# Element-wise steps between GpSimd and VectorE, and the listed order at a layer's end, in a two-layer decoder trunk

## The chip, the core and the metric

One core of one Trainium2 chip runs the whole kernel as one program. The metric is the device time of an execution in microseconds (us). Engines are named as the profile names them: PE is TensorE's matrix multiply, PEld its weight load, DVE VectorE, ACT ScalarE, POOL GpSimd, and SP the engine that issues most of the DMAs.

## What is computed

512 tokens of width 1024 go through two layers. The first mixes tokens by pooling over windows, the second by stick-breaking attention with 16 heads. After each mixer stands a squared-ReLU MLP of width 4096, and every mixer and MLP stands between two RMSNorms. Cut to what matters here:

```python
def rms_norm(x, g):
    return x * lax.rsqrt(jnp.mean(x * x, axis=-1, keepdims=True) + EPS) * g

def sq_relu_mlp(h, w_up, w_down):
    u = jnp.matmul(h, w_up)
    return jnp.matmul(jnp.square(jax.nn.relu(u)), w_down)

for layer in range(2):
    h = rms_norm(x, mix_pre_g[layer])
    m = pool_mixer(h, ...) if layer == 0 else attention(h, k, v) @ w_o
    x = x + rms_norm(m, mix_post_g[layer])
    h = rms_norm(x, mlp_pre_g[layer])
    x = x + rms_norm(sq_relu_mlp(h, w_up[layer], w_down[layer]), mlp_post_g[layer])
    if layer == 0: k, v = split(rms_norm(x, kv_norm_g) @ w_kv)
```

## The kernel before

All products are float32 in three passes: each operand is split into a rounded part (`hi`, a cast on ACT) and the rest (`lo`, a subtraction on DVE), and PE adds hi·hi, hi·lo and lo·hi. So behind nearly every product stand one ACT cast and one DVE subtraction (`split`, line 266, `weight`, line 156).

**The MLP** (`mlp`, from line 575). 32 blocks of 128 hidden channels are made by up products (lines 678 to 680, 24 matmuls a block), squared-ReLU by ACT (lines 596 and 597). 28 of the blocks are taken in five groups of 2, 3, 3, 3 and 3 pairs. Class `Seven` multiplies a group's 2x2 blocks with 7 products in place of 8. Its left operands are blocks `r` and sums of them: four sums per group, made in `left` by GpSimd (line 519). Its right operands are weight halves `w1` and `w2` (the latter in the tile `xn3`) and four combinations `e` and `w12` of them, made in `right` by DVE (line 538). Each product is 18 matmuls for a group of three (line 564), and two additions on DVE take it out of PSUM (line 573). The second half of a group's weights goes into the one tile `xn3` by a DMA of 1.5 MB that waits for the last split of the group before. The last four blocks are multiplied in `contract` (lines 286 to 288, DVE line 426). There each token tile `t` also gets its norm: squares on ACT (line 269), the product with the norm's gain (line 312; of the first 512 columns by GpSimd, of the others by DVE), the sum (line 275) and its power -0.5 on GpSimd (line 282), and the addition to `x` (line 324).

During the first layer's MLP the attention's weights are scaled, split and stored again (`split_apart`, DVE line 216).

**The order.** Where nothing else is said, a scheduler places the instructions of each engine by its own timeline when the program is built; each engine then runs its own queue in that fixed order. Two regions are written by hand for all engines: the pooling (`MIX_ORDER`) and the stretch from the last pair of heads to the second layer's MLP (`END_ORDER`). In `END_ORDER` each word is one step of one engine. `O`, `E`, `F`, `G` are parts of the output projection on PE, with `ov` and `ev` taking them out on DVE (line 1089). `s`, `g`, `V`, `a` are squares (ACT), product with the gain (DVE), factor (DVE line 275, then GpSimd) and addition (DVE) of the first norm; `S`, `W`, `n` the same for the second (`n` is DVE line 363). `t`, `h`, `l` are the transposes (PE), and the split of their result (ACT, DVE line 388). `i`, `k` are the split of an up-weight block 0 to 3 (ACT, DVE line 1139), and `u` is the first half of that block's up product, over token tiles 0 and 1. Digits are the tile and the column half. `ATT_ORDER` lists the attention's steps before: `V` values (24 matmuls a token tile), `P` a pair's queries and keys, `T` transposes, `E1` the hand-written end.

Instructions that the scheduler still owns can be placed between those of a hand-written region: the second layer's first split of `w1` was placed there (line 266).

Of the kernel before, what the change touches and what calls it, by code (L numbers as in the profile page):

```python
# [13 lines left out]
ALU = mybir.AluOpType  # L14
# [18 lines left out]
TS = [slice(t * P, (t + 1) * P) for t in range(T)]  # L33
NS = [slice(0, 512), slice(512, 1024)]
# [24 lines left out]
ATT_ORDER = [  # L59
    (w[0], int(w[1]), [int(c) for c in w[2:]])  # L60
    for w in """V001 K0 V02 P0 V03 S0 P1 T0 V101 S1 A0 P2 T1 V123 A1 S2 P3 T2 O00123 A2 S3 P4 V201 T3 A3
    S4 P5 T4 V223 S5 A4 P6 V301 T5 S6 A5 V323 P7 T6 E1""".split()
]


# [5 lines left out]

END_ORDER = [
    (w if w.startswith("d7") else w.rstrip("0123456789"), [int(c) for c in w if c.isdigit() and not w.startswith("d7")])
    for w in """D6 R0 R1 z01 z00 z02 x00 z11 x02 z12 x01 z10 x12 A60 sc0 x10 y10 A61 y00 oc60 y01 E01 y02 od60 oc61
    mu0 y12 E00 x11 y11 sc1 T01 T02 T00 ah01 O00 ah02 d7h ah00 O01 al01 al00 O10 mu1 O11 ov01 al02 od61
    T12 A70 ah12 ov00 hh6 al12 T11 hl6 T10 ah11 ov11 F00 d7l ah10 al11 O20 oc70 al10 od70 A71 ov20 ov10
    O21 oc71 od71 O30 ov21 hh7 hl7 O31 ov30 G00 ov31 i1 F01 ev00 i0 G01 k1 E11 s00 ev01 R3 F11 g00 s01
    G11 k0 E10 V0 g01 F10 a01 R2 G10 ev11 S01 E20 ev10 s11 a00 s10 F20 g11 G20 S00 V1 g10 E21 ev20 a11
    s20 E31 W0 a10 S11 E30 n01 S10 n00 F30 W1 g20 t01 n11 t00 h01 G30 n10 h00 F31 l01 t10 ev30 G31 h10
    l00 F21 s30 ev31 G21 l10 s31 t11 ev21 h11 g30 s21 l11 i2 V2 u0 V3 g31 i3 a20 a31 S20 a30 S31 u1 g21  # L80
    S30 a21 W3 S21 k2 n31 u2 W2 n30 n21 n20 t30 k3 t21 h30 t20 h21 t31 l30 u3 h20 l21 h31 l20 l31""".split()
]


# [6 lines left out]
def trunk(ctx, tc, x, consts, grow, pw, wup, wdn, wq, wk, wv, wo, out):  # L91
    nc = tc.nc
# [11 lines left out]
    def name(s):  # L104
        uid[0] += 1
        return f"{s}{uid[0]}"

    def ps():
        return psum.tile([P, 512], F32, tag="ps", name=name("ps"))


    xt = [keep.tile([P, D], F32, tag=f"x{t}", name=f"x{t}") for t in range(T)]
# [26 lines left out]
    behind, latest = {}, {}  # L139
# [29 lines left out]
    gate, queue, made, ahead, dn_pool, att_pool = [False], [], {}, 4, [None], [None]  # L169
# [72 lines left out]
    for l in range(2):  # L242
        if l == 1:
            n = len(queue)
# [40 lines left out]
    def mm3(dst, ah, al, bh, bl, start, stop):  # L285
        nc.tensor.matmul(dst, ah, bh, start=start, stop=False)  # L286
        nc.tensor.matmul(dst, ah, bl, start=False, stop=False)  # L287
        nc.tensor.matmul(dst, al, bh, start=False, stop=stop)  # L288
# [9 lines left out]
    class Update:  # L298
# [8 lines left out]
        def squares_of(self, n, y):  # L307
            square_sum(y, self.xn[:, self.cuts[n]], self.st, (0, 1, 4)[n])

        def product(self, n, y, on):  # L310
            cut = self.cuts[n]
            on.tensor_tensor(out=self.scaled[:, cut], in0=y, in1=self.gpost[:, cut], op=ALU.mult)

        def square(self, n, y, on):

            self.squares_of(n, y)
            self.product(n, y, on)

        def first_rstd(self):
            self.r = rstd(self.st, 0, self.eps, third=len(self.cuts) > 2)  # L320
# [11 lines left out]
        def add(self):  # L332
            self.first_rstd()
            for n, cut in enumerate(self.cuts):
                self.add_part(n)
                if self.final:
                    nc.sync.dma_start(out[TS[self.t], cut], xt[self.t][:, cut])
                else:
                    self.squares_of_x(n)

# [62 lines left out]
    def contract(lhs, w, y, first, update=None, tiles=range(T), soon=False):  # L403


        last = len(lhs) - 1
        ups = {}
        for t in tiles:
            up = ups[t] = update(t, y[t]) if update is not None else None
            cuts = up.cuts if up is not None else NS  # L410
            pds = [ps()[:, : cut.stop - cut.start] for cut in cuts]

            def product(n, cs):
                for c in cs:
                    (lh, ll), (wh, wl) = lhs[c], w[c]
                    mm3(
                        pds[n], lh[:, TS[t]], ll[:, TS[t]], wh[:, cuts[n]], wl[:, cuts[n]],
                        c == 0, c == last,
                    )

            def evacuate(n):
                part = y[t][:, cuts[n]]
                if first:
                    nc.scalar.copy(part, pds[n])
                else:
                    nc.vector.tensor_tensor(out=part, in0=pds[n], in1=part, op=ALU.add)
                if up is not None:
                    up.square(n, part, nc.vector if n else nc.gpsimd)

            normed = up is not None and not up.final  # L430
            if t == 0:
                product(0, range(last))
                product(1, range(last))
                product(0, [last])
            else:
                product(0, range(last + 1))
            if normed and t == T - 1 and not soon:
                ups[0].transpose()
            evacuate(0)
            if normed and t > 0:  # L440
                ups[t - 1].rstd()
                ups[t - 1].norm()
            if t == 0:
                product(1, [last])
            elif normed and t == T - 1:
                product(1, [0])
                ups[1].transpose()
                product(1, range(1, last + 1))
            else:
                product(1, range(last + 1))  # L450
                if normed and soon and t == 2:
                    ups[0].transpose()
            evacuate(1)
            for n in range(2, len(cuts)):
                product(n, range(last + 1))
                evacuate(n)
            if up is None:
                fill()
            else:
                up.add()  # L460
                if normed and t == T - 2:
                    behind.update(latest)
        if normed:
            ups[T - 1].rstd()
            ups[T - 1].norm()
            for t in (T - 2, T - 1):
                pending[t] = ups[t]
# [4 lines left out]
    class Seven:  # L472
# [38 lines left out]
        def left(self, i):  # L511

            n, key = self.n, self.PRODUCTS[i][1]
            lo, hi = slice(0, S // 2), slice(S // 2, S)
            r11, r21, r12, r22 = (self.r[:, k, :n, h] for k in range(2) for h in (lo, hi))
            if i == 0:
                self.s1 = self.mp.tile([P, MOST, S // 2], F32, tag="s1", name=name("s1"))
            s1 = self.s1[:, :n]
            sub = lambda out, x, y, op=ALU.subtract: nc.gpsimd.tensor_tensor(out=out, in0=x, in1=y, op=op)  # L519
            if key == "s3":  # L520
                sub(s1, r21, r22, ALU.add)
                sub(r21, r11, r21)
                sub(r11, s1, r11)
            elif key == "r22":
                sub(r11, r12, r11)
            src = {"r11": r11, "s3": r21, "s2": r11, "r22": r22, "s1": s1, "r12": r12, "s4": r11}[key]
            a = self.mp.tile([P, 2, MOST, S // 2], F32R, tag="a", bufs=2, name=name("a"))
            split(src, a[:, 0, :n], a[:, 1, :n])
            return a
# [45 lines left out]
    def mlp(l, mp, update):  # L575

        gate[0] = False
        y = y_tiles()
        firsts = [2 * sum(GROUPS[:g]) for g in range(len(GROUPS))]
        plain = 2 * sum(GROUPS)  # L580
        groups = [Seven(l, firsts[g], n, mp) for g, n in enumerate(GROUPS)]
# [44 lines left out]
        for j, (pu, w) in enumerate(first):  # L626
            up_block(pu, w, slice(S // 2, S))
            up(j, pu)
        for i in range(2):
            groups[0].make(i)  # L630
        for g, group in enumerate(groups):
            coming = groups[g + 1] if g + 1 < len(groups) else None
            if coming:
# [1 line left out]
            ups = list(range(firsts[g + 1], firsts[g + 1] + 2 * GROUPS[g + 1]) if coming else range(plain, NJ))  # L635
# [6 lines left out]
            for i in range(7):  # L642
# [12 lines left out]
                else:  # L655
# [4 lines left out]
                    elif i == 5:  # L660
                        piece = lambda tag, k, bufs=1: mp.tile([P, k, D], F32R, tag=tag, bufs=bufs, name=name("dn"))
                        w, e, x = piece("w1", 3), piece("e", 1), piece("w", 3, 2)
# [5 lines left out]
        w = [get(("dn", l, j)) for j in range(plain, NJ)]  # L668
# [14 lines left out]
    with tc.tile_pool(name="mix0", bufs=1, reuse_waits="tile") as mp:  # L683
# [29 lines left out]
        left, stats, ups, ys, own = {}, {}, {}, {}, {}  # L713
# [100 lines left out]
        def half_up(j):  # L814
# [4 lines left out]
            "z": busy, "r": scale_row, "e": scale_copy, "w": linear, "q": first_squares, "v": first_norm,  # L819
            "b": band, "p": pooled, "c": copied, "f": reached, "m": mixed,  # L820
            "s": lambda t, h: ups[t].squares_of(h, left["m", t, h]),
            "g": lambda t, h: ups[t].product(h, left["m", t, h], nc.vector),
            "V": lambda t: ups[t].first_rstd(), "a": lambda t, h: ups[t].add_part(h),
            "S": lambda t, h: ups[t].squares_of_x(h), "W": lambda t: ups[t].rstd(),
            "n": lambda t, h: ups[t].norm_part(NS[h]), "t": transposes,
# [5 lines left out]
        on = mybir.EngineType  # L831
# [9 lines left out]
    with tc.tile_pool(name="att", bufs=1, reuse_waits="tile") as ap:  # L841
# [79 lines left out]
        for lo, n in SEG.values():  # L921
# [3 lines left out]
                out=d, in_=d, pattern=[[-1, P + c]], base=c - 1, channel_multiplier=1,  # L925
# [136 lines left out]
        vs, os, wos, y = {}, {}, {}, y_tiles()  # L1062
# [6 lines left out]
        def end():  # L1069
# [3 lines left out]
            w = {c: get(("o", c)) for c in range(2, 6)}  # L1073
            bank, o, ups, up = {}, {}, {}, {}
# [66 lines left out]
            def half_up(j):  # L1141
# [12 lines left out]
                "F": lambda t, n: projected("E", t, n, (6,), False, False),  # L1154
                "G": lambda t, n: projected("E", t, n, (7,), False, True), "ev": lambda t, n: added("E", t, n),
                "s": lambda t, n: update(t).squares_of(n, y[t][:, NS[n]]),
                "g": lambda t, n: ups[t].product(n, y[t][:, NS[n]], nc.vector),
                "V": lambda t: ups[t].first_rstd(), "a": lambda t, n: ups[t].add_part(n),
                "S": lambda t, n: ups[t].squares_of_x(n), "W": lambda t: ups[t].rstd(),
                "n": lambda t, n: ups[t].norm_part(NS[n]), "t": transposes,  # L1160
# [4 lines left out]
            on = mybir.EngineType  # L1165
# [91 lines left out]
```

## Time and profile before

| | us |
|---|---|
| median of 3 runs (lowest to highest) | 956.59 (956.35 to 958.49) |
| the profiled execution's own time | 961.12 |
| its span, first to last instruction | 959.3 |
| PE busy | 942.8 |
| DVE busy | 716.0 |
| ACT busy | 568.2 |
| POOL busy | 137.3 |

The first layer's MLP runs from about 45 to 373 us of the span, the attention to about 568, the hand-written end to about 630, and the second MLP to the end. A row of the timeline gives the start, the length, engine, line, operation and tiles, and in brackets the idle time of the engine before it with what ended it. Matmuls overlap: a row of 0.39 us for a matmul over 512 columns stands for a start every 0.227 us, so short losses on PE are read from starts, not from busy time.

### The profile page before, as it was taken

What the parts mean: (1) busy time and instruction counts of PE and PEld (TensorE: products, weight loads), DVE (VectorE), ACT (ScalarE), POOL (GpSimd) and SP (SyncE); (2) the same over time, 40 slices, a digit from 0 to 9 for tenths busy, and PEclk for the clock granted to TensorE, in tenths of its full rate; (3) what the DMA queues carried; (4) which work ended last, traced back from release to release, by engine and by line L of the source; (5) the groups of instructions that cost most, each with busy time, mean ns of one, the idle gap of its engine ahead of it and who ended that gap; (6) DMA issues with size and microseconds to landing.
All of it is one profiled execution on the core that took longest, in us unless ns stands there. A gap on an engine that the chain in (4) does not pass through costs nothing.

```text
span 959.3 us, 12464 instructions
## 1 busy us (share of the span) xinstructions
PE 942.8 (98%) x4757; PEld 801.0 (83%) x4758; DVE 716.0 (75%) x779; ACT 568.2 (59%) x983; POOL 137.3 (14%) x103
## 2 busy tenths in 40 slices
PE   9999999999999999999999999999999999999997
PEld 7998888788788888999899988798888888888885
DVE  5865798997978976476577779964597776857956
ACT  6668879788674747456656554645445454543632
POOL 2220300402303005000000000211030300303003
PEclk9999999999999999999999999999999999999999
DMA  8244879687696860422434271242513333133112
GB/s 311 99 168 165 315 236 354 246 310 288 221 342 242 307 219 1 177 88 88 168 140 174 91 264 47 103 137 82 188 37 132 110 125 117 44 132 110 26 42 88
DMA packets 43406, 156.67 MB, mean 163 GB/s; under 512 B 4305, under 2 KB 4689, under 8 KB 43346
## 3 DMA queue, kind: packets, MB, share of 16 engines
q1 hardware_dynamic: 43346, 155.88, 46.2%
q8 instruction: 37, 0.61, 0.3%
q14 instruction: 23, 0.19, 0.1%
HBM read 122.31 MB, written 33.55 MB: 162 GB/s over the span
## 4 chain that ended last, share of the span: by engine, by line
PE 80%; DVE 9%; DMA 4%; issue 3%; ACT 2%; POOL 1%; POOLq 0%; DVEq 0%; ACTq 0%
PE ps L564 22%; PE ps L680 12%; PE ps L679 12%; PE ps L678 12%; PE ps L286 5%; PE ps L288 5%; PE ps L287 5%; DMA xn<-in_wdn 3%; PE ps L1012 2%; DVE w L266 2%; PE ps L995 1%; PE ps L951 1%; DMA raw<-in_wup 1%; PE ps L952 1%; DVE w L156 1%
## 5 line engine op out<-in xcount | busy, mean ns | idle before, releaser
L564 PE MATMUL ps<-w,a 128*128 128x512 f32 x1176 | 278.8, 390 | 4.3 <-DVE a L266 2.9
L680 PE MATMUL ps<-xnh,w 128*128 128x512 f32 (+1 forms) x712 | 262.1, 369 | 2.3 <-DVE w L1139 2.3
L564 PEld LDWEIGHTS ps<-w,a 128*128 128x128 f32 x1176 | 220.4, 188 | 52.0 <-DVE a L266 4.2
L679 PE MATMUL ps<-xnl,w 128*128 128x512 f32 (+1 forms) x712 | 262.1, 368 | 0.0
L678 PE MATMUL ps<-xnh,w 128*128 128x512 f32 (+1 forms) x712 | 261.6, 369 | 0.0
L680 PEld LDWEIGHTS ps<-xnh,w 128*128 128x128 f32 x712 | 134.7, 189 | 24.7 <-DVE w L1139 2.5
L679 PEld LDWEIGHTS ps<-xnl,w 128*128 128x128 f32 x712 | 134.7, 189 | 22.1 <-DVE xnl L388 0.2
L678 PEld LDWEIGHTS ps<-xnh,w 128*128 128x128 f32 x712 | 134.1, 189 | 21.9
L156 DVE TENSOR_TENSOR w<-raw,w 128x1024 fp32r<-128x1024 f32 x58 | 77.5, 1335 | 63.7 <-ACT w L154 63.5
L154 ACT CAST w<-raw 128x1024 fp32r<-128x1024 f32 x58 | 61.0, 1052 | 82.3 <-PE ps L680 82.2
L573 DVE TENSOR_TENSOR y<-ps,y 128x512 f32<-128x512 f32 x124 | 83.2, 684 | 34.2 <-PE ps L564 34.2
L265 ACT CAST a<-r 128x768 fp32r<-128x768 f32 (+1 forms) x60 | 47.7, 795 | 57.3 <-PE ps L564 39.0
L519 POOL TENSOR_TENSOR s<-r 128x768 f32<-128x768 f32 (+1 forms) x10 | 19.8, 1983 | 371.5 <-ACT r L597 371.5
L265 ACT CAST w<-e 128x1536 fp32r<-128x1536 f32 (+1 forms) x30 | 42.0, 1399 | 51.6 <-DVE e L538 42.3
L266 DVE TENSOR_TENSOR a<-r,a 128x768 fp32r<-128x768 f32 (+1 forms) x60 | 59.4, 993 | 9.0 <-ACT a L265 9.0
L282 POOL TENSOR_TENSOR stat<-stat,mhalf 128x1 f32<-128x1 f32 x32 | 23.6, 739 | 281.2 <-DVE stat L275 279.9
L266 DVE TENSOR_TENSOR w<-e,w 128x1536 fp32r<-128x1536 f32 (+1 forms) x30 | 60.6, 2021 | 3.7 <-ACT w L265 3.4
L519 POOL TENSOR_TENSOR r<-r 128x768 f32<-128x768 f32 (+1 forms) x20 | 49.0, 2452 | 69.9 <-DVE a L266 55.1
L976 DVE TENSOR_TENSOR_SCAN e<-u,begin 128x1280 f32<-128x1280 f32 x16 | 45.2, 2823 | 11.0 <-ACT u L960 10.4
L165 ACT ACTIVATE apart<-apart,eye 128x128 f32<-128x128 f32 (+1 forms) x132 | 42.9, 407 | 0.1
L266 DVE TENSOR_TENSOR w<-w,w 128x1536 fp32r<-128x1536 f32 (+1 forms) x20 | 34.5, 1725 | 6.4 <-ACT w L265 6.4
L266 DVE TENSOR_TENSOR w<-xn,w 128x1536 fp32r<-128x1536 f32 (+1 forms) x20 | 33.0, 1651 | 6.0 <-ACT w L265 6.0
(128 smaller groups left out, 1472.3 us busy)
## 6 DMA issues: line engine op xcount, KB each, us to landing
raw<-in_wup SPq DMA_DIRECT2D x64, 512.0 KB, 4.2
w<-kept SPq DMA_DIRECT2D x60, 512.0 KB, 4.2
kept<-wx SPq DMA_DIRECT2D x30, 512.0 KB, 5.0
w<-in_wdn SPq DMA_DIRECT2D x8, 1536.0 KB, 7.3
kept<-apart SPq DMA_DIRECT2D x24, 512.0 KB, 6.2
xn<-in_wdn SPq DMA_DIRECT2D x8, 1536.0 KB, 8.1
raw<-in_wdn SPq DMA_DIRECT2D x8, 512.0 KB, 4.7
apart<-in_wk SPq DMA_DIRECT2D x7, 512.0 KB, 8.2
```

What stands on the lines that cost most here:

```text
L154: nc.scalar.copy(hi, raw)
L156: nc.vector.tensor_tensor(out=lo, in0=raw, in1=hi.bitcast(F32), op=ALU.subtract)
L265: latest["act"] = nc.scalar.copy(hi, src)
L266: latest["dve"] = nc.vector.tensor_tensor(out=lo, in0=src, in1=hi.bitcast(F32), op=ALU.subtract)
L286: nc.tensor.matmul(dst, ah, bh, start=start, stop=False)
L287: nc.tensor.matmul(dst, ah, bl, start=False, stop=False)
L519: sub = lambda out, x, y, op=ALU.subtract: nc.gpsimd.tensor_tensor(out=out, in0=x, in1=y, op=op)
L564: nc.tensor.matmul(bank, a[:, x, q, TS[t]], w[:, z, q], start=start and q == 0 and k == 0, stop=q == self.n - 1 and k == 2, skip_group_che ...
L573: nc.vector.tensor_tensor(out=part, in0=bank, in1=part, op=ALU.add)
L678: nc.tensor.matmul(pu[:, cols], wh[:, k, :], xnh[:, k, cols], start=k == 0, stop=False)
L679: nc.tensor.matmul(pu[:, cols], wh[:, k, :], xnl[:, k, cols], start=False, stop=False)
L680: nc.tensor.matmul(pu[:, cols], wl[:, k, :], xnh[:, k, cols], start=False, stop=k == KC - 1)
```

## The change

It has six parts.

1. The four sums per group in `left` go from GpSimd to VectorE (40 instructions in both layers).
2. In `contract`, the product with the gain of the first 512 columns goes from GpSimd to VectorE (8 instructions).
3. In `mlp`, the operands of the first two products are made inside `issue_after`: they are placed behind the latest ACT and DVE instructions, which are the splits of the transposes.
4. `END_ORDER` is listed anew with the same steps.
5. `ATT_ORDER`: the values of the last token tile (`V33`) stand behind the queries and keys of the last pair (`P7`).
6. The DMA of the last 256 columns of the output is issued by ACT.

```diff
-    S4 P5 T4 V223 S5 A4 P6 V301 T5 S6 A5 V323 P7 T6 E1""".split()
+    S4 P5 T4 V223 S5 A4 P6 V301 T5 S6 A5 V32 P7 V33 T6 E1""".split()
...
-    G11 k0 E10 V0 g01 F10 a01 R2 G10 ev11 S01 E20 ev10 s11 a00 s10 F20 g11 G20 S00 V1 g10 E21 ev20 a11
...
-    S30 a21 W3 S21 k2 n31 u2 W2 n30 n21 n20 t30 k3 t21 h30 t20 h21 t31 l30 u3 h20 l21 h31 l20 l31""".split()
...
+    ev20 t10 l11 s20 F21 ev31 h10 G21 g20 i3 ev21 l10 s21 l01 s31 V2 g21 u0 g31 a20 a21 S20 V3 k2 S21 u1
+    a30 W2 S30 a31 n21 S31 u2 n20 W3 k3 n31 t20 t21 n30 h20 t31 h21 l20 t30 h31 u3 l21 h30 l31 l30""".split()
...
-            on.tensor_tensor(out=self.scaled[:, cut], in0=y, in1=self.gpost[:, cut], op=ALU.mult)
+            nc.vector.tensor_tensor(out=self.scaled[:, cut], in0=y, in1=self.gpost[:, cut], op=ALU.mult)
...
-                    nc.sync.dma_start(out[TS[self.t], cut], xt[self.t][:, cut])
+                    queue = nc.scalar if n == 2 else nc.sync
+                    queue.dma_start(out[TS[self.t], cut], xt[self.t][:, cut])
...
-                    up.square(n, part, nc.vector if n else nc.gpsimd)
+                    up.square(n, part)
...
-            sub = lambda out, x, y, op=ALU.subtract: nc.gpsimd.tensor_tensor(out=out, in0=x, in1=y, op=op)
+            sub = lambda out, x, y, op=ALU.subtract: nc.vector.tensor_tensor(out=out, in0=x, in1=y, op=op)
...
-        for i in range(2):
-            groups[0].make(i)
+        with tc.issue_after(latest["act"].ins), tc.issue_after(latest["dve"].ins):
+            for i in range(2):
+                groups[0].make(i)
```

The scheduler's order moves with it. The first place is DVE in the first layer's MLP, at the start of the third group, whose blocks are `r_1093`. `e_1551` is the combination for its second product (the rows begin with its split) and `a_1593` the left operand of that product. Before:

```order
L266 TENSOR_TENSOR w_1597<-e_1551,w_1597 128x1536
L573 TENSOR_TENSOR y_529<-ps_1601,y_529 128x512
L216 TENSOR_TENSOR spare_1503<-spare_1503,wx_536 128x1024
L538 TENSOR_TENSOR e_1551<-e_1551,w_1329 128x1536
L573 TENSOR_TENSOR y_530<-ps_1602,y_530 128x512
L266 TENSOR_TENSOR a_1593<-r_1093,a_1593 128x768
```

Now (line 520 is a sum, 574 and 539 are what 573 and 538 were):

```order
L266 TENSOR_TENSOR w_1597<-e_1551,w_1597 128x1536
L216 TENSOR_TENSOR spare_1503<-spare_1503,wx_536 128x1024
L520 TENSOR_TENSOR r_1093<-r_1093 128x3x256
L574 TENSOR_TENSOR y_529<-ps_1601,y_529 128x512
L574 TENSOR_TENSOR y_530<-ps_1602,y_530 128x512
L539 TENSOR_TENSOR e_1551<-e_1551,w_1329 128x1536
L520 TENSOR_TENSOR r_1093<-s_1547,r_1093 128x3x256
L156 TENSOR_TENSOR w_1542<-raw_1543,w_1542 128x1024
L266 TENSOR_TENSOR a_1593<-r_1093,a_1593 128x768
```

Two sums and one weight split have come between the two operands of the product; the first sum, `s_1547`, stands three rows ahead of this piece. On PE, between the product's first four matmuls, which need `w_1597`, and its other fourteen, which need `a_1593`, stood 12 matmuls of up products, and now stand 32.

The second place is DVE in the hand-written end, from the last projection part to the split of up-weight block 2 (line 1139, now 1142). `y_3176` and `x_72` belong to tile 2, `y_3177` and `x_73` to tile 3; line 1089 is now 1092 and line 388 now 389. Before:

```order
L1089 TENSOR_TENSOR y_3176<-ps_5462,y_3176 128x512
L312 TENSOR_TENSOR y_3177<-y_3177,grow_4148 128x512
L388 TENSOR_TENSOR xnl<-ps_5543,xnh 128x4x128
L275 TENSOR_SCALAR stat_5471<-stat_5471 128x1
L275 TENSOR_SCALAR stat_5535<-stat_5535 128x1
L312 TENSOR_TENSOR y_3177<-y_3177,grow_4148 128x512
L324 SCALAR_TENSOR_TENSOR x_72<-y_3176,stat_5471,x_72 128x512
L324 SCALAR_TENSOR_TENSOR x_73<-y_3177,stat_5535,x_73 128x512 x2
L312 TENSOR_TENSOR y_3176<-y_3176,grow_4148 128x512
L266 TENSOR_TENSOR w_5851<-w_5718,w_5851 128x1024
L324 SCALAR_TENSOR_TENSOR x_72<-y_3176,stat_5471,x_72 128x512
L1139 TENSOR_TENSOR w_5553<-raw_5432,w_5553 128x1024
```

Now:

```order
L1092 TENSOR_TENSOR y_3176<-ps_5505,y_3176 128x512
L389 TENSOR_TENSOR xnl<-ps_5533,xnh 128x4x128
L389 TENSOR_TENSOR xnl<-ps_5492,xnh 128x4x128
L275 TENSOR_SCALAR stat_5539<-stat_5539 128x1
L312 TENSOR_TENSOR y_3176<-y_3176,grow_4148 128x512
L312 TENSOR_TENSOR y_3177<-y_3177,grow_4148 128x512
L324 SCALAR_TENSOR_TENSOR x_72<-y_3176,stat_5539,x_72 128x512 x2
L275 TENSOR_SCALAR stat_5503<-stat_5503 128x1
L1142 TENSOR_TENSOR w_5522<-raw_5475,w_5522 128x1024
```

The weight split of the MLP (line 266) has left the piece and now stands behind the splits of the last transposes, block 2's split has come ahead of tile 3's additions, and two splits of transposes (line 389) stand behind the last projection part where one stood before. On PE the last projection part was followed by four transposes and then block 0's up product, which now follows directly.

More of the change, by code (lines that the diff above doesn't have):

```diff
@@ L73 @@
     (w if w.startswith("d7") else w.rstrip("0123456789"), [int(c) for c in w if c.isdigit() and not w.startswith("d7")])
[L74 to L77, printed above, removed]
-    G11 k0 E10 V0 g01 F10 a01 R2 G10 ev11 S01 E20 ev10 s11 a00 s10 F20 g11 G20 S00 V1 g10 E21 ev20 a11
-    s20 E31 W0 a10 S11 E30 n01 S10 n00 F30 W1 g20 t01 n11 t00 h01 G30 n10 h00 F31 l01 t10 ev30 G31 h10
-    l00 F21 s30 ev31 G21 l10 s31 t11 ev21 h11 g30 s21 l11 i2 V2 u0 V3 g31 i3 a20 a31 S20 a30 S31 u1 g21
-    S30 a21 W3 S21 k2 n31 u2 W2 n30 n21 n20 t30 k3 t21 h30 t20 h21 t31 l30 u3 h20 l21 h31 l20 l31""".split()
+    for w in """D6 R0 R1 z02 z01 z00 x02 z12 x01 x00 O00 x12 y00 sc0 y02 A60 y01 y12 A61 oc60 ov00 E11 oc61 od60
+    od61 z10 mu0 z11 x10 E00 x11 hh6 sc1 T01 y10 T02 y11 T00 ah02 E01 ah00 d7h ah01 O01 al00 mu1 O10
+    al02 al01 T11 T10 ov10 ah11 A70 ov01 ah10 al10 T12 O11 al11 ah12 d7l al12 hl6 A71 ov11 oc70 F11 od70
+    oc71 O20 od71 hh7 F00 hl7 F01 ov20 G11 G01 ev11 G00 ev01 s11 E10 ev00 s01 g11 s00 F10 g01 G10 V0 g00
+    O21 ev10 a01 s10 O30 a00 S01 g10 O31 S00 ov30 W0 V1 E30 ov21 i0 n00 i1 F30 a11 t00 k0 S11 G30 E20
+    h00 ev30 R2 l00 F20 a10 E31 n01 S10 ov31 t01 W1 G20 k1 s30 E21 h01 n11 R3 g30 t11 i2 F31 n10 G31 h11
+    ev20 t10 l11 s20 F21 ev31 h10 G21 g20 i3 ev21 l10 s21 l01 s31 V2 g21 u0 g31 a20 a21 S20 V3 k2 S21 u1
+    a30 W2 S30 a31 n21 S31 u2 n20 W3 k3 n31 t20 t21 n30 h20 t31 h21 l20 t30 h31 u3 l21 h30 l31 l30""".split()
 ]
@@ L308, in squares_of, with product, square @@
             square_sum(y, self.xn[:, self.cuts[n]], self.st, (0, 1, 4)[n])
-        def product(self, n, y, on):
+        def product(self, n, y):
             cut = self.cuts[n]
-            on.tensor_tensor(out=self.scaled[:, cut], in0=y, in1=self.gpost[:, cut], op=ALU.mult)
-        def square(self, n, y, on):
+            nc.vector.tensor_tensor(out=self.scaled[:, cut], in0=y, in1=self.gpost[:, cut], op=ALU.mult)
+        def square(self, n, y):
             self.squares_of(n, y)
-            self.product(n, y, on)
+            self.product(n, y)
         def first_rstd(self):
@@ L821, in trunk @@
             "s": lambda t, h: ups[t].squares_of(h, left["m", t, h]),
-            "g": lambda t, h: ups[t].product(h, left["m", t, h], nc.vector),
+            "g": lambda t, h: ups[t].product(h, left["m", t, h]),
             "V": lambda t: ups[t].first_rstd(), "a": lambda t, h: ups[t].add_part(h),
@@ L1156, in end @@
                 "s": lambda t, n: update(t).squares_of(n, y[t][:, NS[n]]),
-                "g": lambda t, n: ups[t].product(n, y[t][:, NS[n]], nc.vector),
+                "g": lambda t, n: ups[t].product(n, y[t][:, NS[n]]),
                 "V": lambda t: ups[t].first_rstd(), "a": lambda t, n: ups[t].add_part(n),
```

## The prediction

> **What bounds the kernel now.** I read the page's first parts, then the chain of waits, then busy time by stretch, then single rows at the losses. The page's first row looks saturated:
>
> ```profile
> PE 942.8 (98%) x4757; PEld 801.0 (83%) x4758; DVE 716.0 (75%) x779; ACT 568.2 (59%) x983; POOL 137.3 (14%) x103
> ```
>
> A busy PE need not be at its pace, so I look at starts. The chain merges runs of matmuls that nothing held up:
>
> ```profile
> 64.34 2.72 PE ps L564 x12
> ```
>
> That is 0.227 us per matmul over 512 columns, the pace almost everywhere. Moving other engines' work can therefore win only what PE loses between starts. Busy time by stretch (the second number is PE's, then PEld, DVE, ACT, POOL) says where:
>
> ```profile
> 150.00:200.00 50.00, 48.44 (x213) 39.46 (x212) 45.70 (x38) 41.83 (x77) 11.41 (x4) 1.00 0.80 300
> 200.00:250.00 50.00, 48.40 (x213) 39.38 (x211) 40.95 (x35) 36.46 (x65) 8.35 (x3) 1.00 0.80 284
> 250.00:310.00 60.00, 59.22 (x260) 48.72 (x260) 50.98 (x44) 42.10 (x63) 15.60 (x4) 1.00 0.79 280
> 310.00:352.00 42.00, 41.62 (x184) 34.47 (x184) 37.72 (x37) 26.04 (x30) 1.85 (x1) 1.00 0.90 312
> 568.00:600.00 32.00, 31.59 (x171) 26.80 (x170) 29.53 (x39) 18.52 (x40) 0.00 (x0) 1.00 0.22 74
> 615.00:650.00 35.00, 32.68 (x237) 31.35 (x236) 24.20 (x33) 18.11 (x33) 6.80 (x7) 0.95 0.36 121
> 650.00:930.00 280.00, 280.00 (x1237) 231.91 (x1236) 204.42 (x189) 139.47 (x164) 42.30 (x18) 1.00 0.29 96
> ```
>
> PE stands idle 1.56 + 1.60 + 0.78 + 0.38 = 4.3 us in the first layer's MLP, 0.4 us where the attention's end begins and 2.3 us before the second MLP, and never in the second MLP. The first stage's idle time is five waits, all for DVE:
>
> ```profile
> 181.13 0.39 PE L564 MATMUL ps<-w,a 128*128 128x512 f32 x1
> 181.93 0.97 PE L564 MATMUL ps<-w,a 128*128 128x512 f32 x3 [0.40 <-DVE w L266]
> 182.73 0.40 PE L678 MATMUL ps<-xnh,w 128*128 128x512 f32 x1
> 186.80 1.43 PE L564 MATMUL ps<-w,a 128*128 128x512 f32 x5 [1.15 <-DVE a L266]
> 245.91 0.98 PE L564 MATMUL ps<-w,a 128*128 128x512 f32 x3 [1.02 <-DVE w L266]
> 250.78 0.50 PE L564 MATMUL ps<-w,a 128*128 128x512 f32 x1 [1.36 <-DVE a L266]
> 310.43 1.88 PE L564 MATMUL ps<-w,a 128*128 128x512 f32 x7 [0.38 <-DVE a L266]
> ```
>
> A wait costs more than its idle time: from 181.13 to 182.73 four matmuls took 1.60 where 0.91 would do, 0.69 lost beside 0.40 idle. With 0.3 more for each of the five, this stage loses about 5.8 us.
>
> **Sums on VectorE, in the first MLP.** Here are DVE, from the landing of the second weight half to the operand that released PE at 186.80, and GpSimd's three sums beside it:
>
> ```profile
> 170.68 1.76 DVE L538 TENSOR_TENSOR e<-xn,w 128x1536 f32<-128x1536 f32 x1 [1.23 <-DMA xn<-in_wdn]
> 172.35 2.88 DVE L156 TENSOR_TENSOR w<-raw,w 128x1024 fp32r<-128x1024 f32 x1
> 175.15 3.40 DVE L538 TENSOR_TENSOR w<-w 128x1536 f32<-128x1536 f32 x1
> 178.47 1.28 DVE L573 TENSOR_TENSOR y<-ps,y 128x512 f32<-128x512 f32 x2
> 179.67 2.20 DVE L266 TENSOR_TENSOR w<-e,w 128x1536 fp32r<-128x1536 f32 x1
> ...
> 182.40 1.21 DVE L216 TENSOR_TENSOR spare<-spare,wx 128x1024 f32<-128x1024 f32 x1
> 183.53 1.74 DVE L538 TENSOR_TENSOR e<-e,w 128x1536 f32<-128x1536 f32 x1
> ...
> 185.80 1.81 DVE L266 TENSOR_TENSOR a<-r,a 128x768 fp32r<-128x768 f32 x2
> ```
>
> ```profile
> 172.00 2.15 POOL L519 TENSOR_TENSOR s<-r 128x768 f32<-128x768 f32 x1 [40.97 <-ACT r L597]
> 174.23 2.71 POOL L519 TENSOR_TENSOR r<-r 128x768 f32<-128x768 f32 x1
> 177.01 3.24 POOL L519 TENSOR_TENSOR r<-s,r 128x768 f32<-128x768 f32 x1
> ```
>
> While GpSimd works, DVE's operations on SBUF stretch: 2.88 us for 1024 columns that take 1.21 alone, 3.40 and 2.20 for 1536 that take 1.74. That is 1.67 + 1.66 + 0.46 = 3.8 us given away in one group; the reads of PSUM (0.64 each) do not stretch. On DVE a sum has the shape of the left operand's split, whose undisturbed row is:
>
> ```profile
> L266 DVE TENSOR_TENSOR a<-s,a 128x768 fp32r<-128x768 f32 x8 | 7.6, 950 | 0.5 <-ACT a L265 0.5
> ```
>
> Three sums cost 2.85 us in this stretch, the fourth 0.95 later. So DVE is not loaded more: it gains 3.8 and pays 3.8 per group. What moves is the order. Until `w_1597` is done, DVE now has 1.76 + 0.68 + 1.22 + 0.95 + 0.68 + 1.74 + 1.74 = 8.8 us, some 8.3 as starts overlap by 0.08 each; it was 181.87 - 170.68 = 11.2. The wait at 181.93 has 2.9 us of room. From the start of `w_1597` to the end of `a_1593` the order shows 1.74 + 1.21 + 0.95 + 2 x 0.68 + 1.74 + 0.95 + 1.22 + 0.95 = 10.1, 9.5 with the overlap, against 186.75 - 179.67 = 7.1: 2.4 longer. But PE has 32 matmuls there in place of 12, 20 x 0.227 = 4.5 us more. The wait of 1.15 turns into some 0.95 us of room. The later boundaries are built alike. I leave 1.5 us of the 5.8, since the room is thin and a late landing of the weights shifts everything behind it: **-4.3 us**, with bounds 0 and -5.8. If DVE did not shorten without GpSimd, the sums would stand unhidden (rivals).
>
> In the second MLP PE never waits and DVE is busy 204 of 280 us; 20 sums add at most 20 x 0.95 = 19 us, which PE's 280 us of matmuls cover: 0. The first splits moved behind the transposes are covered in the same way, by the up products of blocks 0 to 3 that follow them: 0 there, and what they free is counted next.
>
> **End region.** Before:
>
> ```profile
> 620.94 1.22 DVE L266 TENSOR_TENSOR w<-w,w 128x1024 fp32r<-128x1024 f32 x1
> 622.08 0.75 DVE L324 SCALAR_TENSOR_TENSOR x<-y,stat,x 128x512 f32<-128x512 f32 x1
> 622.74 0.21 DVE L275 TENSOR_SCALAR stat<-stat 128x1 f32<-128x1 f32 x1
> 622.87 1.22 DVE L1139 TENSOR_TENSOR w<-raw,w 128x1024 fp32r<-128x1024 f32 x1
> ```
>
> ```profile
> 621.54 0.28 PE L679 MATMUL ps<-xnl,w 128*128 128x256 f32 x1
> 624.14 0.39 PE L680 MATMUL ps<-xnh,w 128*128 128x256 f32 x1 [2.32 <-DVE w L1139]
> ```
>
> ```profile
> 625.50:629.00 3.50, 3.50 (x19) 3.50 (x19) 3.06 (x4) 0.06 (x1) 0.97 (x1) 0.52 0.37 138
> ```
>
> PE waits for block 2's weight split, which stands behind the MLP's split and an addition: 2.60 us between starts where 0.12 is the pace. Then the granted clock (third number from the end) is 0.52 for 3.5 us, another 1.7 lost. The waits of 1.0 to 1.4 us in the MLP were followed by a clock of 1.00. Together 2.5 + 1.7 + about 0.1 = 4.3 us.
>
> [...]
>
> Now, from the end of the last projection part, with the same rows' lengths: DVE takes it out by 0.9 us, then does tile 1's split, by 1.5 (both 0.6 apart); block 0's second matmul needs that split and waits 1.4 us, since the transposes that stood between are gone. PE then has three up products of 24 x 0.12 = 2.9 us, until about 10.1. Block 2's split is done at 6.0, ahead of its use at 7.2. Tile 2's norm is done at 9.3, ahead of the transposes; tile 3's at 11.2 and 11.85, behind a factor that takes 1.25 us through GpSimd, so PE waits about 0.6 more. Sum 2.0 us in waits below 1.5, each with a full clock: **-2.3 us**, bounds 0 and -4.3.
>
> **Attention's last pair.** Scores wait for a split of the queries that stands behind other splits:
>
> ```profile
> 571.58 0.41 PE L951 MATMUL ps<-k,q 128*128 128x384 f32 x1 [0.41 <-DVE q L908]
> ```
>
> With the 24 value matmuls (2.9 us) behind the queries this is covered: **-0.5**, bounds 0 and -0.7.
>
> **Products with the gain, and the last DMA.** Eight products of about 0.69 us come to DVE in the two `contract` calls. At the very end:
>
> ```profile
> 951.36 0.42 DVE L426 TENSOR_TENSOR y<-ps,y 128x256 f32<-128x256 f32 x1
> 952.30 0.42 DVE L426 TENSOR_TENSOR y<-ps,y 128x256 f32<-128x256 f32 x1 [0.52 <-PE ps L288]
> ```
>
> The one for the last tile goes into the 0.52 us of idle time and pushes the last read of PSUM by up to 0.2. The DMA moved to ACT no longer stands behind the one before it on SP, about as much. Net 0, bounds -0.2 and +0.2.
>
> **Sum.** -4.3 - 2.3 - 0.5 = -7.1 us. The profiled execution took 961.1 (span 959.3 and 1.8 around it), so 954.0. The median shown is 4.5 us below that execution; I carry the difference: **949.5 us**.
>
> **Rivals.**
> - The waits in the first MLP stay, because the landing sets them and not the sums. For it: the row at 170.68 starts on a DMA. Against it: the 16 us from there to 186.75 hold 3.8 us of stretching. Then -2.8: 953.8. Chance 0.13.
> - The slow clock is not the wait's doing and stays: 1.7 us less gain, 951.2. Against it: the stretches shown from 150 to 600 and from 650 to 930 have a clock of 1.00 throughout, and only the one with the long wait does not. Chance 0.05.
> - The new order waits elsewhere and eats the gain, mostly on ACT's casts, which now wait for DVE's sums (ACT is busy 41.8 of 50 us at 150): about 956. Chance 0.07.
> - Slower: DVE becomes the bound in the first MLP. If its operations do not shorten with GpSimd idle, four sums, 3.8 us, stand unhidden at each of the three boundaries that wait now: 11.4 - 2.8 = +8.6, 965. It decides once a boundary's DVE work exceeds its old 16.1 us by more than PE's 4.5 us of new cover. Chance 0.09, since the stretched and unstretched rows lie side by side.
>
> **Chances and range.** The forecast's case has 0.66, between 945.9 (every loss named gone: 5.8 + 4.3 + 0.6 = 10.7) and 952.5. About 0.3%, 2.9 us, is what a measurement of this kernel can tell from no change, so faster means below 953.7: 0.66 + 0.05 and half of the first rival, 0.77. Within: the other half and the third rival, 0.14. Slower: 0.09. The range 945.9 to 956.6 leaves out the last rival and little else.
>
> **What would show it.** Right: no DVE row of 1024 columns above 1.3 us in the first MLP, PE idle there below 1.5 us, no stretch near 0.5 clock around 625, a wait of about 1.4 us at block 0's second matmul, PE still without idle time in the second MLP. Wrong: DVE rows as long as before, waits of PE for `w` or `a` that add up to more than 4 us, or a wait above 2 us in the end region with a low clock behind it.

## The result, and the profile after

| | median of 9, us (lowest to highest) | against before, 95% interval |
|---|---|---|
| before | 957.75 (956.35 to 959.62) | |
| after | 961.63 (959.64 to 964.26) | 1.0041 (1.0027 to 1.0056) |

The change makes the kernel slower by 0.4%, where 949.5 us was predicted. The profiled execution of after took 960.48 us, with a span of 958.7. The first row of its page and busy time by stretch (length, then PE, PEld, DVE, ACT, POOL, granted clock, DMA share, GB/s) against the same stretches of before:

```profile
PE 942.5 (98%) x4757; PEld 800.9 (84%) x4758; DVE 714.0 (74%) x827; ACT 568.5 (59%) x983; POOL 28.6 (3%) x55
```

```profile
150.00:200.00 50.00, 48.13 (x213) 39.53 (x212) 45.08 (x43) 40.15 (x74) 0.00 (x0) 1.00 0.79 297
200.00:250.00 50.00, 50.00 (x223) 41.39 (x222) 41.38 (x39) 40.09 (x71) 0.00 (x0) 1.00 0.83 294
250.00:310.00 60.00, 60.00 (x266) 49.71 (x265) 50.66 (x49) 41.17 (x61) 0.00 (x0) 1.00 0.82 288
310.00:352.00 42.00, 42.00 (x187) 34.75 (x187) 34.70 (x39) 22.97 (x29) 0.00 (x0) 1.00 0.77 278
568.00:600.00 32.00, 29.53 (x142) 24.45 (x141) 24.48 (x32) 13.42 (x31) 0.93 (x1) 0.95 0.19 71
615.00:650.00 35.00, 32.66 (x241) 30.52 (x240) 27.52 (x38) 19.41 (x36) 4.83 (x4) 1.00 0.39 137
650.00:930.00 280.00, 280.00 (x1237) 231.86 (x1236) 201.86 (x205) 138.64 (x163) 0.00 (x0) 1.00 0.28 96
```

Three of the four stretches of the first MLP are full now, and the second MLP still is. The first stretch has somewhat more idle time than before (1.87 us against 1.56), and the end of the attention (568 to 600) lost 2.1 us of busy time more, with a clock of 0.95. PE's rows name two new waits. The first is at the third group's second product:

```profile
182.98 1.20 PE L565 MATMUL ps<-w,a 128*128 128x512 f32 x4 [1.87 <-ACT a L265]
```

The second is in `O00`, the first step of the output projection, whose last two weight tiles are still on their way:

```profile
568.50 0.39 PE L288 MATMUL ps<-w,ohl 128*128 128x512 f32 x1
570.61 0.49 PE L286 MATMUL ps<-w,ohl 128*128 128x512 f32 x1 [1.73 <-DMA w<-kept]
571.85 0.62 PE L287 MATMUL ps<-w,ohl 128*128 128x512 f32 x1 [0.74 <-DMA w<-kept]
```

The clock is halved behind it:

```profile
572.00:575.50 3.50, 3.50 (x12) 3.01 (x13) 0.69 (x1) 0.27 (x1) 0.00 (x0) 0.51 0.00 0
```

To compare executions I use **PE's lost time**: over all pairs of successive matmuls, the distance of their starts, less the median distance for matmuls of that line and shape. It takes in idle time, the pace after it and a slow clock. Of before there are two profiles, the one of the prediction and one of an unchanged copy (the first experiment):

| lost in, us | before, 961.12 | before again, 956.47 | after, 960.48 |
|---|---|---|---|
| third group of the first MLP (160 to 200) | 2.11 | 0.12 | 2.10 |
| fourth (235 to 265) and fifth (295 to 330) | 3.63 | 1.27 | -0.09 |
| 350 to 400 | 0.50 | 0.52 | 1.05 |
| 550 to 600 | 1.37 | 1.41 | 4.97 |
| 600 to 650 | 4.67 | 4.35 | 3.52 |
| sum | 12.28 | 7.67 | 11.55 |

The sums differ as the times do: 12.28 - 7.67 = 4.6 of 4.65, and 11.55 - 7.67 = 3.9 of 4.0. So these rows hold nearly all of the difference.

### The profile page after: what moved, and what is told of

Its sections match the earlier page's. It is cut to its first block, busy times and chain, and to the rows that moved or that the text cites. A ratio compares the mean times of both kernels' runs of the same rounds, so it can differ in the third digit from the quotient of the medians.

```text
span 958.7 us, 12446 instructions
## 1 busy us (share of the span) xinstructions
PE 942.5 (98%) x4757; PEld 800.9 (84%) x4758; DVE 714.0 (74%) x827; ACT 568.5 (59%) x983; POOL 28.6 (3%) x55
## 4 chain that ended last, share of the span: by engine, by line
PE 92%; DVE 3%; issue 1%; POOL 1%; ACT 1%; DMA 1%; POOLq 0%; DVEq 0%; SPq 0%
PE ps L565 28%; PE ps L681 14%; PE ps L682 14%; PE ps L683 14%; PE ps L286 4%; PE ps L287 4%; PE ps L288 4%; PE ps L1015 2%; PE ps L998 1%; POOL stat L282 1%; PE ps L954 1%; PE ps L955 1%; PE ps L376 1%; DMA w<-kept 1%; PE ps L794 1%
## 5 line engine op out<-in xcount | busy, mean ns | idle before, releaser
L156 DVE TENSOR_TENSOR w<-raw,w 128x1024 fp32r<-128x1024 f32 x58 | 70.8, 1221 | 58.1 <-ACT w L154 58.0
L266 DVE TENSOR_TENSOR a<-r,a 128x768 fp32r<-128x768 f32 (+1 forms) x60 | 53.9, 899 | 11.0 <-ACT a L265 11.0
L266 DVE TENSOR_TENSOR w<-e,w 128x1536 fp32r<-128x1536 f32 (+1 forms) x30 | 49.4, 1646 | 2.4 <-ACT w L265 2.2
L269 ACT ACTIVATE xn<-y 128x512 f32<-128x512 f32 (+1 forms) x25 | 15.4, 614 | 39.3 <-DVE y L427 33.0
L286 PE MATMUL ps<-w,xnh 128*128 128x256 f32 x128 | 36.5, 286 | 0.8 <-ACT xnh L385 0.8
```

The source lines that it names most:

```text
L156: nc.vector.tensor_tensor(out=lo, in0=raw, in1=hi.bitcast(F32), op=ALU.subtract)
L266: latest["dve"] = nc.vector.tensor_tensor(out=lo, in0=src, in1=hi.bitcast(F32), op=ALU.subtract)
```

## Experiments

For runs 1 to 4, theory A holds that every execution of before has the losses that its profile showed, and that the change loses by a new wait at `O00`; rival B holds that these losses are not ordinary. From run 5 on, theory A takes in what runs 1 and 2 showed: most executions of before do not have the losses of the first MLP in that size, and the change adds waits, mostly at `O00`. The other rivals stand in the expectations. Each run's ratio is to before on the same chip, with its interval.

**1. Before, unchanged.**

> The kernel before, unchanged. Theory A (the profile of before shows losses that every execution has, and the loss of the change is a new wait at O00, the first projection part of the new list, for its weight load): ratio 1.000, and a second profile loses about 5.8 us in the first MLP and 4.3 us in the end region again. Rival B (that profiled execution, 3.4 us above the median, was not an ordinary one): ratio 1.000, and a second profile, if its time is near 957.5, loses 3 to 4 us less in one of these two places.

957.47 us, ratio 1.0001 (0.9990 to 1.0013); profiled at 956.47. Rival B holds for the first MLP, and theory A for the end region: the first MLP lost 1.4 us in place of 5.7 (4.35 less, somewhat more than B's 3 to 4), the end region nearly the same (table above). The row that differs is a DMA's: kilobytes, and us from issue to landing, of the third group's second weight half. In the prediction's profile, then in this one:

```profile
xn<-in_wdn SPq DMA_DIRECT2D x1, 1536.0 KB, 10.7
```

```profile
xn<-in_wdn SPq DMA_DIRECT2D x1, 1536.0 KB, 9.3
```

The first DVE row of the chain behind it starts at once here, where before it showed 1.23 us of idle time on that DMA:

```profile
169.20 1.76 DVE L538 TENSOR_TENSOR e<-xn,w 128x1536 f32<-128x1536 f32 x1
```

Over all seven profiled kernels with the sums on GpSimd (before, and runs 1, 3, 7, 8, 9, 10), sorted by that landing:

| | 1 | 3 | 10 | 8 | before | 9 | 7 |
|---|---|---|---|---|---|---|---|
| issue to landing, us | 9.28 | 9.46 | 9.87 | 10.06 | 10.71 | 10.96 | 11.74 |
| third group lost, us | 0.12 | 0.26 | 0.69 | 0.90 | 2.11 | 2.41 | 3.17 |

The order is the same in both rows: what the third group loses goes with the landing, whatever else is changed (a relation over seven executions; no run was made to move the landing itself). The fourth group agrees: landings of 9.0 to 9.4 us with 0.5 to 0.8 lost, 10.1 with 2.7 and 10.4 with 3.0.

**2. Before, with the sums on VectorE alone** (line 519).

```diff
-            sub = lambda out, x, y, op=ALU.subtract: nc.gpsimd.tensor_tensor(out=out, in0=x, in1=y, op=op)
+            sub = lambda out, x, y, op=ALU.subtract: nc.vector.tensor_tensor(out=out, in0=x, in1=y, op=op)
```

> Before with one change: the four sums per group on VectorE. Theory A: the waits of the first MLP go, -4 us, ratio 0.994 to 0.997. Rival B (those waits are not in an ordinary execution of before): ratio 0.998 to 1.001. Rival C (the sums load VectorE and make new waits): above 1.002.

957.21 us, ratio 0.9987 (0.9974 to 1.0001): B's range. The waits of the fourth and fifth group are gone, and the wait of 2.03 us (by starts) at the third is there as in after. It is an order on ACT. Of after, the rows around it:

```profile
173.97 2.45 ACT L165 ACTIVATE apart<-apart,eye 128x128 f32<-128x128 f32 x8
181.15 1.04 ACT L154 CAST w<-raw 128x1024 fp32r<-128x1024 f32 x1 [4.73 <-PE ps L683]
182.10 0.83 ACT L265 CAST a<-r 128x768 fp32r<-128x768 f32 x1
```

The sum that makes the left operand `a` is on DVE, in the same profile:

```profile
178.84 0.95 DVE L520 TENSOR_TENSOR r<-r 128x768 f32<-128x768 f32 x1
```

So `a` is ready for its cast since 179.8, but the cast stands behind the cast of an up-weight, whose tile PE itself holds until its last up product. So PE finishes, then ACT casts twice (1.04 and 0.83), and only then PE goes on: a wait of 2.03 us in six of the six profiles of this order (runs 2, 4, 5, 6 and 11, and after). The weights landed in 8.8 to 9.4 us in these six, so no late landing made it.

**3. Before, with the new list of the end region alone.** The edit is the `END_ORDER` of the change.

> Before with one change: the new list of the end region, but the old order of the attention. Theory A: O00 waits less than 1 us here, because with V33 ahead of P7 the weight loads for the projection are spread and the last one lands about 4.7 us after the first transposes, when O00 needs it at about 4.6; block 2's wait and the slow clock behind it go: -2 us, ratio 0.997 to 0.999. Rival D (the new list itself is slower, whatever the attention's order): ratio above 1.002, O00 waits over 2 us with a clock near 0.5 behind it.

958.26 us, ratio 1.0008 (0.9996 to 1.0019). Neither theory's range: `O00` does not wait, as A said, but the gain of 2 us is not there. The end region loses 4.51 us: 1.37 at block 0's second matmul, 0.95 and 1.45 at the last transposes. The wait for block 2 was exchanged for others. The MLP's first split (line 266) still stands among tile 3's additions here, since the list alone does not move it.

**4. After, with the old list of the end region.**

> After with the old list of the end region alone. Theory A: O00's waits and slow clock (4.9 us) go, block 2's come back (2 us): about 3 us below after, near 957 to 958 by the medians of this chip or ratio 0.996 to 1.000 against before. Rivals B and C (the sums bring nothing, or cost): it stays at 1.002 or above.

956.64 us, ratio 0.9983 (0.9971 to 0.9995). As A said, and 5 us below after; block 2's wait came back at 1.46 us only (run 10 shows why).

**5. After, with the old order of the attention.**

```diff
-    S4 P5 T4 V223 S5 A4 P6 V301 T5 S6 A5 V32 P7 V33 T6 E1""".split()
+    S4 P5 T4 V223 S5 A4 P6 V301 T5 S6 A5 V323 P7 T6 E1""".split()
```

> After with the old order of the attention (V33 ahead of P7). Theory A (O00 waits because V33 behind P7 frees the tiles of the projection's weights in one burst, so that three pairs of loads are queued and the last lands 7.7 us after the first transposes where O00 wants it at 4.6; with the old order it lands at 4.7): O00's wait falls below 1 us, no slow clock at 572, time about 957.5, ratio 0.998 to 1.002. Theory D (the new list of the end region does it, by where it puts O00): the wait of 2 to 3 us and the slow clock stay, ratio above 1.003.

956.99 us, ratio 1.0000 (0.9988 to 1.0012): theory A; D falls. The list is still the new one, and PE goes through `O00` without a wait:

```profile
569.62 0.40 PE L288 MATMUL ps<-w,ohl 128*128 128x512 f32 x1
569.86 0.39 PE L286 MATMUL ps<-w,ohl 128*128 128x512 f32 x1
570.09 0.40 PE L287 MATMUL ps<-w,ohl 128*128 128x512 f32 x1
```

The cause is the weight loads (line 226), each of which waits until PE has released the tile. In the DMA issues from 564.2 us on, the last pair needs 6.7 us in after, and 3.8 here:

```profile
w<-kept SPq DMA_DIRECT2D x2, 512.0 KB, 6.7
```

```profile
w<-kept SPq DMA_DIRECT2D x2, 512.0 KB, 3.8
```

In after the 24 value matmuls of `V33` end the stage. They release three pairs of tiles within 3 us (issues at 561.4, 562.9 and 564.3), and 3 MB queue up, one load landing every 1.2 to 2 us, the last at 571.81. With `V33` ahead of `P7` the last three pairs are issued at 553.8, 559.3 and 564.7, and the last lands at 569.33. `O00` asks for it 4.6 us after the transposes' start, at 568.7 in after.

**6. After, with `O00` moved behind `A61` in the new list.**

```diff
-x01 x00 O00 x12 y00 sc0 y02 A60 y01 y12 A61 oc60 ov00 E11
+x01 x00 x12 y00 sc0 y02 A60 y01 y12 A61 oc60 O00 ov00 E11
```

> After with the step O00 moved behind A61 in the new list, both orders else new. Theories A and D: O00 finds its weights landed; the 4.9 us in 568 to 580 go unless A60 (whose left operands were made while PE waited) waits in its place; time 957 to 958.5, ratio 0.999 to 1.002. Rival E (the 4.9 us are A60's, O00 only hides them): PE waits for ACT or DVE at A60 by 2 us or more, ratio above 1.003.

958.65 us, ratio 1.0007 (0.9996 to 1.0017). A60 does not wait, `O00` by 0.38 us: rival E falls. With runs 3 and 5: the new list waits at `O00` only together with the new order of the attention, and the pair costs 3.6 us in the profile (4.97 against 1.41).

**7. Before, with `V33` behind `P7` alone** (the reverse of run 5's edit).

> Before with one change: V33 behind P7. The old list's first projection step comes later, so theory A says: the wait for the queries' split (0.57 us at 567) goes, no new wait at the projection, ratio 0.999 to 1.000. Theory D': the change of the attention's order costs by itself: ratio above 1.002.

956.46 us, ratio 0.9996 (0.9983 to 1.0008). The 0.57 us wait for the queries' split is gone, no new one at the projection; D' falls.

**8. After, with the sums on GpSimd again** (the reverse of run 2's edit).

> After with the four sums per group on GpSimd again. Theory A (in an ordinary execution the sums on VectorE take 1.1 us of waits away in the first MLP and add one of 2.0 us in the third group, where ACT's cast of the left operand now stands behind a weight cast that waits for PE): the wait near 183 goes, 1.1 us come back near 247 and 306, about 1 us faster than after: ratio 1.002 to 1.004. Rival (the sums gain 4 us, as predicted): slower than after by 3 us or more, ratio above 1.007.

960.78 us, ratio 1.0035 (1.0021 to 1.0049): A's range, and the rival is out. The interval overlaps after's own, so which of the two is faster is not settled by time. The wait at 183 is gone, `O00`'s is there, and the first MLP loses 4.5 us: 0.9 in the third group, and 3.6 in the fourth and fifth, where 1.1 was expected. The landings of the third and fourth group were 10.06 and 10.10 us in this execution.

**9. Before, with the first 512 columns' product with the gain on VectorE.**

```diff
-                    up.square(n, part, nc.vector if n else nc.gpsimd)
+                    up.square(n, part, nc.vector)
```

> Before with one change: in the last four blocks of an MLP the product with the gain of the first 512 columns on VectorE. Theory A: the wait of PE for ACT's cast of the first layer's normed x near 380 us grows from 0.40 to 0.94 us, which every kernel with this part shows so far; nothing else: +0.5 us, ratio 0.999 to 1.002. The prediction's term (0, from -0.2 to +0.2): the wait stays 0.40.

957.97 us, ratio 1.0003 (0.9988 to 1.0018). By time this can't be told from nothing, but PE's wait for ACT's cast (line 384) at the end of the first layer's MLP grew from 0.40 to 0.94 by starts, as in each profile that has this part and in none that lacks it.

**10. Before, with the first operands behind the transposes' splits.** The edit is the `issue_after` of the change.

> Before with one change: the first operands of the second product pair behind the transposes' splits. Theory A: block 2's weight split no longer stands behind the MLP's first split on VectorE, so the wait near 620 falls from 2.47 to about 1.46 us, as in the run of after with the old list: -1.0 us or somewhat more, where the slow clock goes with it: ratio 0.997 to 0.9995. Rival: another split takes its place, ratio 1.000.

955.40 us, ratio 0.9970 (0.9957 to 0.9984): the one part that gains by itself. Block 2's weight split stands directly behind the additions now, since the MLP's first split (1.22 us) is no longer between them:

```profile
617.22 0.75 DVE L324 SCALAR_TENSOR_TENSOR x<-y,stat,x 128x512 f32<-128x512 f32 x1
617.89 0.20 DVE L275 TENSOR_SCALAR stat<-stat 128x1 f32<-128x1 f32 x1
618.01 1.22 DVE L1141 TENSOR_TENSOR w<-raw,w 128x1024 fp32r<-128x1024 f32 x1
```

```profile
619.28 0.39 PE L682 MATMUL ps<-xnh,w 128*128 128x256 f32 x1 [1.31 <-DVE w L1141]
```

PE's wait fell from 2.47 us (by starts) to 1.47 and the clock stayed at 1.00: 1.0 us, and 0.9 to 1.3 more in an execution where the clock would have fallen (last section). What else the 2.9 us of the ratio (1.5 to 4.1) hold was not told apart. The new list removes this wait in another way and pays elsewhere (run 3), so the two parts do not add.

**11 and 12. Towards a version that beats both.** Run 11 is after with the old list and the product on GpSimd again.

> After with the old list of the end region and the first 512 columns' product on GpSimd again: what stays is the sums on VectorE, the first operands behind the transposes, V33 behind P7 and the last DMA on ACT. Theory A: 0.5 us below the run with the old list alone, waits 2.03 us at 183, 0.40 at 380 and 1.46 at 621; ratio 0.996 to 0.999.

Run 12 leaves two of the four sums on VectorE (`sup` is the same operation on GpSimd):

```diff
                 sub(s1, r21, r22, ALU.add)
                 sub(r21, r11, r21)
-                sub(r11, s1, r11)
+                sup(r11, s1, r11)
             elif key == "r22":
-                sub(r11, r12, r11)
+                sup(r11, r12, r11)
```

> The same, with only the first two sums of a group on VectorE and the other two on GpSimd. By the order of ACT the left operand's cast of the second product then stands ahead of the weight cast in the third group too. Theory A (ACT's order makes the 2.03 us wait at 183): that wait goes, waits of VectorE at the group boundaries may come back by up to 1 us; fastest of all, 954 to 955, ratio 0.994 to 0.998. Rival (the wait at 183 is VectorE's load, not ACT's order): a wait of 1.5 us or more stays there, no faster than the run beside it.

Run 11: 954.40 us, ratio 0.9969 (0.9957 to 0.9982), with the waits as expected (2.03, 0.40, 1.47). Run 12: **952.65 us, ratio 0.9940 (0.9925 to 0.9956)**, faster than before and than after. On its ACT the cast of `a` stands ahead of the up-weight's:

```profile
180.34 0.83 ACT L265 CAST a<-r 128x768 fp32r<-128x768 f32 x1 [3.33 <-DVE r L520]
181.74 1.06 ACT L154 CAST w<-raw 128x1024 fp32r<-128x1024 f32 x1 [0.56 <-PE ps L684]
```

PE's row behind it has no wait, and neither has any other in the first MLP:

```profile
181.53 1.07 PE L566 MATMUL ps<-w,a 128*128 128x512 f32 x4
```

So the wait at 183 was ACT's order. Run 12 by itself does not rule out VectorE's load, since it takes two sums off VectorE too; the rows of after do (run 2), where the sum was done 2.3 us before the cast began.

## Why the prediction was wrong, step by step

It missed by 961.6 - 949.5 = 12.1 us. By its own terms, against the same profiled execution of before (the last row: the profiled execution of after lies 1.15 us below its median, and what the median execution loses beyond it is not shown), 12.0 of it are found:

| term | predicted | shown | share of the miss |
|---|---|---|---|
| profiled execution to median | -4.5 | 0 | 4.5 |
| waits in the first MLP | -4.3 | -3.7 | 0.6 |
| end region (600 to 650) | -2.3 | -1.2 | 1.1 |
| attention's last pair and `O00` (550 to 600) | -0.5 | +3.6 | 4.1 |
| products with the gain | 0 | +0.55 | 0.55 |
| after's profile to its median | 0 | +1.15 | 1.15 |

- **From the profiled execution to the median.** The step that failed first: "I carry the difference". That execution was 4.5 us above the median of three shown, and 3.4 above the median of nine. Against run 1's profile, which is 4.65 us faster and near the median, it lost 4.35 us more in the first MLP, where two landings were later. So the sum took the same loss off twice, once as the sums' gain and once as the offset. The row that warned was there (the 1.23 us of idle time on the DMA), and was the first rival's ground, with 0.13; its 953.8 carried the same offset.
- **Sums on VectorE.** Right: DVE's rows no longer stretch. Rows of 1024 columns between 45 and 373 us now read

```profile
L156 DVE TENSOR_TENSOR w<-raw,w 128x1024 fp32r<-128x1024 f32 x28 | 34.2, 1220 | 16.5 <-ACT w L154 16.5
```

  where before had a mean of 1397, and DVE is busy 2 us less with 48 operations more. The waits of the fourth and fifth group went. Wrong: the third group kept 2.1 us, by the mechanism that the third rival had (0.07), though not for want of the sum: the cast waited for another cast in front of it. I followed DVE's order row by row and did not follow ACT's: the product's first four matmuls need, beside `w_1597`, the cast of `a_1593` (ACT's line 265 releases them at 182.98), and neither my walk nor the piece of order shown above has it.
- **End region.** The wait at block 0's second matmul was 1.37 us, forecast 1.4, and the clock near 625 is full, so the second rival fell. The transposes of tile 3 cost 1.6 in place of 0.6: each of its two factors took 1.8 us from its row on DVE to the row that uses it (620.53 to 622.32, and 625.62 to 627.40), where my walk has 1.25, and so both of its norm's rows come about 1 us later. Half of the gain, then, against this one profile. The 1.7 us for the slow clock were too much: five profiles have the old wait of 2.47 us, in three of them the clock fell and cost 0.9 to 1.3 us, and in the two others, runs 2 and 7, the region lost 3.4 us, no more than the 3.5 of after. With the moved splits the old list loses 2.4 (runs 4, 10 and 11), so beside them the new list costs about 1 us; alone it gains nothing (run 3).
- **Attention's last pair.** The wait went, as forecast. What failed is what the step left out: `V33` behind `P7` moves the release of tiles for weight loads, and the new list puts `O00`, which needs those tiles, 4.6 us behind. I did not look at SP's queue there.
- **Products with the gain.** The term was taken at 0 for work beside other work. At the end of the first layer's MLP PE waits for that chain already, and nothing is beside it: 0.55.
- **The last DMA.** As forecast: from the last matmul's end to the end of the span 7.1 us before, 7.2 after.

## What to carry to other kernels

Before a loss in one profile is booked as a gain, ask whether other executions have it: a wait that starts on a DMA's landing may not be there next time (here the load took 10.7 us in one execution of before and 9.3 in another, and the third group lost 2.11 us and 0.12), and if the profiled execution lies above the median, its extra losses are the first suspects for that very difference. When an order changes, follow each operand that PE waits for through every queue it passes (the cast's, the loads'), with what stands ahead of it there. Parts that are harmless or good alone can hurt together (the two orders here) or take away the same wait (the list and the moved splits), so they are worth trying in pairs.

## What the hardware showed beside this

The slow clock does not follow from the wait's length alone. In the profiles of before, after and these runs PE sat idle 1.7 to 2.3 us thirteen times at three places (block 2, the third group, `O00`); behind six of them the clock fell to between 0.51 and 0.66 for the next 3.5 us, behind seven it stayed at 1.00. The same wait at block 2, in runs 9 and 7 (idle 2.32 and 2.31 us):

```profile
622.60:626.10 3.50, 3.50 (x20) 3.50 (x19) 3.02 (x6) 0.00 (x0) 0.99 (x2) 0.55 0.48 150
```

```profile
622.50:626.00 3.50, 3.50 (x30) 3.19 (x28) 3.00 (x6) 0.45 (x1) 1.01 (x2) 1.00 0.46 150
```

In the clock records of before and of after the slow stretch is at 0.50 for 3.41 us; the 0.52 and 0.51 that their windows of 3.5 us show are means. What lets the clock fall behind one of these waits and not behind another of the same length is not shown by any run.

A slow stretch added 1.6 us to the loss of the third group (3.7 in runs 4 and 6 against 2.1), 1.4 at `O00` (4.97 in after against 3.60 in run 8) and 0.9 to 1.3 at block 2 (in before, runs 1 and 9, against runs 2 and 7). So the waits of 1.7 to 2.3 us had a price here that changed from execution to execution.

What makes the same 1.5 MB load land in 9.3 us once and in 11.7 another time is not shown by any run. In the seven profiles with two or all of the sums on VectorE the third group's load landed in 8.8 to 9.4 us, and in the seven with all of them on GpSimd in 9.3 to 11.7; whether the place of the sums moves the landing was not tested.
